# Chaining the transfer of E behind its batch's last tile transfer on the SyncE queue

## The chip, the cores and the metric

The kernel runs on one core of one Trainium2 chip, as one program in one launch. The metric is device time in microseconds (us): the median of several runs of one build. A profiled execution of the same program supplies the trace that is read below. Five engines work side by side: TensorE (PE; its weight loads are shown apart as PEld), VectorE (DVE), ScalarE (ACT), GpSimd (POOL) and SyncE (SP). In this kernel SP issues nearly all transfers, one after the other, in the order that the program was scheduled in; an issue whose semaphores are not yet there holds up every issue behind it.

## The reference

One layer of a hybrid decoder on 1056 tokens (1024 of a prompt, 32 of a sample group): a SwiGLU half, a mixing block (windowed attention beside a diagonal state-space model, the SSM), and a second SwiGLU half.

```python
x = x + 0.5 * swiglu(rms_norm(x, p['ffn1_norm']), p['ffn1_w1'], p['ffn1_w3'], p['ffn1_w2'])
h = rms_norm(x, p['mix_norm'])
...
y_ssm, new_re, new_im = s5_scan(u, s_re, s_im, p['ssm_a_re'], p['ssm_a_im'], p['ssm_log_dt'],
                                p['ssm_b_re'], p['ssm_b_im'], p['ssm_c_re'], p['ssm_c_im'], p['ssm_d'])
...
x = x + merged @ p['w_out']
x = x + 0.5 * swiglu(rms_norm(x, p['ffn2_norm']), p['ffn2_w1'], p['ffn2_w3'], p['ffn2_w2'])
```

The SSM has 32 groups of 64 complex states. Its discretised matrices depend on parameters alone, not on the tokens, so the kernel can work them out long before the scan needs them.

## The kernel before, in words

Each SwiGLU half is an up stage and a down stage. The up stage (`up`, lines 365 to 418) walks over 22 blocks of 128 hidden columns, f = 0 to 21 (the first two in another form, so the loop runs from f = 2). For each f, `wload` (282) asks SP for the weights `in_w3a` and `in_w1a` (line 286, two transfers each, into tiles `wr`), DVE forms sums of them (`ws`, `wr`), ACT casts the high parts (`wh`, line 301) and DVE the low parts (`wl`). PE then runs seven products for each of two column halves, 168 matmuls per f (line 232, into banks `P`), and DVE and ACT combine the results in tiles `e`; sums of them go to memory through `hs` (line 357). The down stage (`down`, 448) reads them back as `hl`.

The SSM's parameters are worked out inside the up stage of the first half, in NB = 8 batches, by the generator `params_b` (598 to 677). `hook` (681) drives it: at the end of f = 4, 6, ..., 18 it starts a batch, and its first part runs on POOL alone, behind a load of `tb` from `in_bc` (line 608). POOL forms B (in `ta`), C (in `tb`), and E, a table of powers that fills the right half of `ta` and is the last thing of the batch. Two f later, ahead of the last product of that f, the second part runs: PE transposes B (`ptr`, 638), ACT copies it to `mt` and SP stores that in `pa_d` (640); ACT copies C to `c` (647) and `cp` (652, stored by 653); PE multiplies (`pk`, 659); ACT copies to `kt` (662); eight small transfers spread `kt` into `tz` (672); ACT copies `tz` to `tp` (674), the batch's last tile; and two transfers store `tp` and E (`ta[:, 512:1024]`) in the left and right half of `pb_d` (675, 677). `pa_d` and `pb_d` are read by the scan, after the first half has ended.

What sets the order: each engine's instructions are put in order when the program is built, by a scheduler with its own timeline, which may place an instruction ahead of one that was written earlier. `tc.issue_after(ins)` adds an edge "behind ins in issue order" to the instructions of the block that run on the engine of `ins`, and to no others. Here `ins` is an ACT copy and the block holds only an SP transfer. `in_order(engine)` (142) chains the instructions of the block on the named engine one behind the other in issue order, without a wait for the end of any. It holds only instructions traced inside the block. The tiles `ta`, `tb`, `e`, `hl` and most others come from one pool of 34 buffers (NT); a new tile takes a buffer when its earlier reader or writer is through.

Of the kernel before, what the change touches and what calls it, by code (L numbers as in the profile page):

```python
# [46 lines left out]
def body(tc, I, O):  # L47
    nc = tc.nc
    V, S, Pl, PE = nc.vector, nc.scalar, nc.gpsimd, nc.tensor
    dma = nc.sync.dma_start  # L50
    mark = {}
    es = ExitStack()
    with es:
# [24 lines left out]
        def bank(pool_, name):  # L78
            p, n = psum[pool_]
            t = p.tile([128, n, 512] if n > 1 else [128, 512], F32, tag=pool_, name=name)  # L80
            return t
# [41 lines left out]
        def PP(shape, name, dt=F32):  # L123
            return pp_p.tile(shape, dt, tag="pp", name=name)
# [16 lines left out]
        @contextmanager  # L141
        def in_order(*engines, last=None):

            traced = nc.cur_bb.bb.instructions
            first = traced[-1]
            yield
            start = next(k for k in reversed(range(len(traced))) if traced[k] is first) + 1
            last = {} if last is None else last
            for i in traced[start:]:
                if i.engine in [e.engine for e in engines or (PE, V, S)]:  # L150
                    if i.engine in last:
                        tc.add_manual_dep(i, last[i.engine].name, mybir.DependencyInfo(
                            mybir.DependencyClass.NoSync, mybir.DependencyReason.DATA), reason="in_order")
                    last[i.engine] = i
# [345 lines left out]
        pb_d = dr.tile([NB, 128, 1024], F32, name="pb_d")  # L500
# [97 lines left out]
        def params_b(b):  # L598
# [69 lines left out]
            tz = PP([128, 4, 128], "tz")  # L668
# [2 lines left out]
            for j in range(8):  # L671
                dma(tv[:, j, :, j * 16:128], ktg[:, :, 0:(8 - j) * 16])
            tp = PP([128, 4, 16, 8], "tp")
            last = S.copy(tp, tz.rearrange("p g (j c) -> p g c j", j=8)).ins
            dma(pb_d[b, :, 0:512], tp.rearrange("p g c j -> p (g c j)"))
            with tc.issue_after(last):
                dma(pb_d[b, :, 512:1024], ta[:, 512:1024])

        todo, plast = [], {}
# [1 line left out]
        def hook(f, end):  # L681

            if not end:
                if f > 4 and f % 2 == 0:
                    with tc.issue_after(mark["pe"]):
                        next(todo.pop(), None)
                return
            if f == 2:
                with tc.issue_after(mark["hid"]):
                    load_consts()  # L690
                with tc.issue_after(mark["up"]):
                    params()
            elif f > 3 and f % 2 == 0 and f < 4 + 2 * NB:
                todo.append(params_b((f - 4) // 2))
                with in_order(Pl, last=plast):
                    next(todo[-1])
# [203 lines left out]
        for m0 in (0, 2):  # L900
# [5 lines left out]
            for c in range(NC):  # L906
                p = bank("pp", "pu")
# [706 lines left out]
```

## Time and profile before

| | us |
|---|---|
| median of 3 runs | 2124.15 |
| lowest, highest run | 2118.39, 2124.85 |
| the profiled execution, its own time | 2122.6 |
| its span, first to last instruction | 2120.8 |
| PE busy | 2041.1 (96%) |
| DVE busy | 1510.3 (71%) |
| ACT busy | 819.9 (39%) |
| POOL busy | 333.1 (16%) |

The 1.8 us between the profiled execution's time and its span lie outside the program's instructions. A busy PE is not a PE at its peak, since the duration of a matmul depends on the granted clock. "SPq" is SP's sequencer, that is, the queue of issues; the duration of an issue is not that of the transfer, and a DMA in the chain of waits is the transfer itself from issue to landing.

### The profile page before, as it was taken

The numbers are of one execution on the slowest core, as the hardware profiler recorded it, in microseconds if no ns is written. First come the engines' busy times: TensorE is split into PE (matmuls) and PEld (weight loads), VectorE is DVE, ScalarE is ACT, GpSimd is POOL, SyncE is SP. The second block draws the span as 40 slices with busy tenths as digits, with TensorE's granted clock in tenths as the row PEclk, the third lists the DMA queues.
The fourth block names the chain that finished last, engine by engine and source line by source line (L and its number), as shares of the span: only waits on it lengthen the run. The fifth ranks groups of instructions, "written<-read, shape, count | busy, mean of one in ns | idle before, by whom it ended". The sixth has DMA issues, their size and how long they took to land.

```text
span 2120.8 us, 39645 instructions
## 1 busy us (share of the span) xinstructions
PE 2041.1 (96%) x15588; PEld 2009.0 (95%) x15588; DVE 1510.3 (71%) x2566; ACT 819.9 (39%) x1569; POOL 333.1 (16%) x719
## 2 busy tenths in 40 slices
PE   8898989999999999999999899998999999999999
PEld 7898989998899999999999799988999999999999
DVE  5886766766477775767877856779777777756774
ACT  4432433333344452235555642344332232333342
POOL 0009777766000000320000200000000000000000
PEclk9899999999999999999999999999999999999999
DMA  4142333334777774652322274431432322377884
GB/s 164 36 150 99 117 100 100 100 115 143 269 260 258 266 270 142 204 167 64 91 77 97 80 264 141 136 104 40 152 106 77 122 91 92 103 263 245 301 281 159
DMA packets 155833, 320.64 MB, mean 151 GB/s; under 512 B 28592, under 2 KB 60144, under 8 KB 155632
## 3 DMA queue, kind: packets, MB, share of 16 engines
q1 hardware_dynamic: 155648, 318.12, 44.3%
q8 instruction: 122, 2.00, 0.4%
q14 instruction: 63, 0.52, 0.1%
HBM read 231.13 MB, written 84.07 MB: 149 GB/s over the span
## 4 chain that ended last, share of the span: by engine, by line
PE 75%; POOL 8%; DVE 7%; DMA 4%; issue 3%; ACT 2%; SPq 1%; DVEq 0%; ACTq 0%; POOLq 0%
PE P L232 27%; PE D L232 19%; PE pj L232 11%; POOL tb L84 6%; PE pm L232 4%; PE p L232 3%; PE pu L232 2%; PE Q L232 2%; POOL ta L84 2%; DMA hl<-hc 1%; DVE wl L84 1%; PE ss L735 1%; DVE B L96 1%; DMA tb<-in_bc 1%; DMA wr<-in_w1a 1%
## 5 line engine op out<-in xcount | busy, mean ns | idle before, releaser
L232 PE MATMUL P<-Xh,wh 128*128 128x264 f32 x2240 | 647.0, 289 | 38.0 <-DVE e L84 29.8
L232 PE MATMUL P<-Xl,wh 128*128 128x264 f32 x2240 | 644.6, 288 | 0.0
L232 PE MATMUL P<-Xh,wl 128*128 128x264 f32 x2240 | 641.9, 287 | 0.0
L232 PEld LDWEIGHTS P<-Xh,wh 128*128 128x128 f32 x2240 | 429.3, 192 | 44.1 <-DVE e L84 19.5
L232 PEld LDWEIGHTS P<-Xl,wh 128*128 128x128 f32 x2240 | 429.2, 192 | 1.7 <-issue 1.7
L232 PEld LDWEIGHTS P<-Xh,wl 128*128 128x128 f32 x2240 | 428.8, 191 | 0.2 <-issue 0.2
L232 PE MATMUL D<-hh,wh 128*128 128x264 f32 x1232 | 349.9, 284 | 1.9 <-DVE e L84 1.8
L232 PE MATMUL D<-hl,wh 128*128 128x264 f32 x1232 | 350.2, 284 | 0.7 <-DVE hl L84 0.7
L232 PE MATMUL D<-hh,wl 128*128 128x264 f32 x1232 | 349.1, 283 | 0.7 <-DVE wl L84 0.7
L84 DVE TENSOR_TENSOR wl<-wr,wh 128x512 fp32r<-128x512 f32 (+1 forms) x426 | 289.0, 694 | 60.9 <-ACT wh L301 41.8
L211 ACT CAST wh<-wr 128x512 fp32r<-128x512 f32 (+1 forms) x266 | 154.1, 606 | 317.2 <-DVE wr L84 158.4
L84 DVE TENSOR_TENSOR e<-e,P 128x528 f32<-128x528 f32 (+1 forms) x250 | 169.7, 680 | 116.2 <-PE P L232 85.6
L232 PEld LDWEIGHTS D<-hh,wh 128*128 128x128 f32 x1232 | 231.9, 188 | 2.5 <-ACT wh L211 1.4
L232 PEld LDWEIGHTS D<-hh,wl 128*128 128x128 f32 x1232 | 231.5, 188 | 1.3 <-DVE wl L84 1.3
L232 PEld LDWEIGHTS D<-hl,wh 128*128 128x128 f32 x1232 | 231.6, 188 | 1.1 <-DVE hl L84 1.1
L301 ACT CAST wh<-wr 128x512 fp32r<-128x512 f32 x160 | 98.9, 620 | 275.5 <-PE P L232 264.7
L232 PE MATMUL pj<-xh,wh 128*128 128x352 f32 x528 | 172.1, 326 | 3.0 <-DVE gt L84 3.0
L232 PE MATMUL pj<-xl,wh 128*128 128x352 f32 x528 | 171.4, 325 | 0.0
L232 PE MATMUL pj<-xh,wl 128*128 128x352 f32 x528 | 171.1, 324 | 0.0
L301 ACT CAST wh<-ws 128x512 fp32r<-128x512 f32 x120 | 74.4, 621 | 222.3 <-PE P L232 214.5
L84 DVE TENSOR_TENSOR wr<-wr 128x512 f32<-128x512 f32 (+1 forms) x140 | 123.8, 885 | 31.2 <-DMA wr<-in_w2b 15.6
L84 DVE TENSOR_TENSOR hl<-hl,hh 128x1056 fp32r<-128x1056 f32 x84 | 97.6, 1162 | 33.8 <-ACT hh L427 33.7
(608 smaller groups left out, 3698.8 us busy)
## 6 DMA issues: line engine op xcount, KB each, us to landing
hl<-hc SPq DMA_DIRECT2D x70, 528.0 KB, 5.6
wr<-in_w2a SPq DMA_DIRECT2D x60, 512.0 KB, 5.2
wr<-in_w2b SPq DMA_DIRECT2D x60, 512.0 KB, 4.7
hc<-hs SPq DMA_DIRECT2D x110, 264.0 KB, 3.1
wr<-in_w_in SPq DMA_DIRECT2D x26, 512.0 KB, 3.5
hc<-e SPq DMA_DIRECT2D x42, 264.0 KB, 3.5
wr<-in_w3a SPq DMA_DIRECT2D x40, 256.0 KB, 3.0
wr<-in_w1a SPq DMA_DIRECT2D x40, 256.0 KB, 4.7
```

What stands on the lines that cost most here:

```text
L84: e.tensor_tensor(out=o, in0=a, in1=b, op=op)
L96: V.scalar_tensor_tensor(out=o, in0=a, scalar=s, in1=b, op0=op0, op1=op1)
L211: S.copy(h[:, 0:m, :], r[:, i:i + m, :])
L232: mark["pe"] = PE.matmul(ps, a, b, start=first and i == 0, stop=last and i == 2, **kw).ins
L301: S.copy(h, s)
L735: PE.matmul(ps, f32(ones), s[:, kk, :], start=a + i + kk == 0, stop=a == 1 and i + kk == 2)
```

## The change

The two stores of a batch are put into a block that chains SP's instructions: first the store of `tp`, then that of E. The hold on ACT's copy, which named no SP instruction, is gone.

```diff
             tp = PP([128, 4, 16, 8], "tp")
-            last = S.copy(tp, tz.rearrange("p g (j c) -> p g c j", j=8)).ins
-            dma(pb_d[b, :, 0:512], tp.rearrange("p g c j -> p (g c j)"))
-            with tc.issue_after(last):
+            S.copy(tp, tz.rearrange("p g (j c) -> p g c j", j=8))
+            with in_order(nc.sync):
+                dma(pb_d[b, :, 0:512], tp.rearrange("p g c j -> p (g c j)"))
                 dma(pb_d[b, :, 512:1024], ta[:, 512:1024])
```

Two places of SP's queue show what moves. The first is ahead of the weights of f = 7, where batch 0 is at work; the semaphores that an issue waits for stand in brackets, among them one DMAHW, that of the transfer eight places earlier. Before (`ta_1733` is batch 0's E, `mt` its first stored tiles):

```order
L357 DMA hc1_136<-hs_2047 128x528 [waits DMAHW5_49,DVE_49]
L677 DMA pb_d_124<-ta_1733 128x512 [waits DMAHW6_49,Pool_49]
L286 DMA wr_3017<-in_w3a 128x512 [waits DMAHW7_49,DVE_49]
L286 DMA wr_3017<-in_w3a 128x512 [waits DMAHW0_49]
L640 DMA pa_d_123<-mt_2252 128x256 [waits DMAHW1_49,Activation_49]
L640 DMA pa_d_123<-mt_2258 128x256 [waits DMAHW2_49,Activation_49]
L286 DMA wr_3016<-in_w1a 128x512 [waits DMAHW3_49,DVE_49]
```

With the change:

```order
L357 DMA hc1_136<-hs_2047 128x528 [waits DMAHW5_49,DVE_49]
L286 DMA wr_3017<-in_w3a 128x512 [waits DMAHW6_49,DVE_49]
L286 DMA wr_3017<-in_w3a 128x512 [waits DMAHW7_49]
L640 DMA pa_d_123<-mt_2252 128x256 [waits DMAHW0_49,Activation_49]
L640 DMA pa_d_123<-mt_2258 128x256 [waits DMAHW1_49,Activation_49]
L286 DMA wr_3016<-in_w1a 128x512 [waits DMAHW2_49,DVE_49]
```

Batch 0's E, with its wait for POOL, has left the place ahead of the weights of f = 7 and of batch 0's own `pa_d` stores.

The second place is the end of batch 0, ahead of the weights of f = 8 (`ta_2336` is batch 1's E, `tb_2940` the load that opens batch 2). Before:

```order
L675 DMA pb_d_124<-tp_2302 128x512 [waits DMAHW0_49,Activation_49]
L286 DMA wr_3257<-in_w3a 128x512 [waits DMAHW1_49,DVE_49]
L286 DMA wr_3257<-in_w3a 128x512 [waits DMAHW2_49]
L677 DMA pb_d_124<-ta_2336 128x512 [waits DMAHW3_49,Pool_49]
L286 DMA wr_3256<-in_w1a 128x512 [waits DMAHW4_49,DVE_49]
L286 DMA wr_3256<-in_w1a 128x512 [waits DMAHW5_49]
L357 DMA hc4_134<-hs_2613 128x528 [waits DMAHW6_49,DVE_49]
L405 DMA hc5_138<-e_2455 128x528 [waits DMAHW7_49,DVE_49]
L608 DMA tb_2940<-in_bc 128x128 [waits DMAHW0_49]
```

With the change:

```order
L676 DMA pb_d_124<-tp_2302 128x512 [waits DMAHW7_49,Activation_49]
L677 DMA pb_d_124<-ta_1733 128x512 [waits DMAHW0_49,Pool_49]
L286 DMA wr_3257<-in_w3a 128x512 [waits DMAHW1_49,DVE_49]
L286 DMA wr_3257<-in_w3a 128x512 [waits DMAHW2_49]
L286 DMA wr_3256<-in_w1a 128x512 [waits DMAHW3_49,DVE_49]
L286 DMA wr_3256<-in_w1a 128x512 [waits DMAHW4_49]
L357 DMA hc4_134<-hs_2613 128x528 [waits DMAHW5_49,DVE_49]
L405 DMA hc5_138<-e_2455 128x528 [waits DMAHW6_49,DVE_49]
L608 DMA tb_2940<-in_bc 128x128 [waits DMAHW7_49,DMAHW0_49]
```

Batch 1's E no longer stands ahead of batch 2's load; batch 0's does, behind `tp` of batch 0. That load also waits for DMAHW0 now, E's own landing, since its tile takes over the buffer that E was read from. So it goes on to the last batch: before, the E that is issued near `tp` of a batch is that of the next batch, which POOL is still working on; with the change it is that batch's own. POOL's order is the same in both; PE, DVE and ACT change by a few neighbouring places near f = 21 and in the attention.

## Rows read from the trace of the kernel before

**Rows 1.** The page's chain that ended last: share of the span by engine.

```profile
PE 75%; POOL 8%; DVE 7%; DMA 4%; issue 3%; ACT 2%; SPq 1%; DVEq 0%; ACTq 0%; POOLq 0%
```

**Rows 2.** Windows: length, busy us (count) of PE PEld DVE ACT POOL, PEclk, DMA, GB/s.

```profile
239.77:284.81 45.04, 45.04 (x369) 44.24 (x368) 32.51 (x49) 18.38 (x38) 33.74 (x74) 1.00 0.31 101
...
205.84:555.71 349.87, 322.92 (x2532) 315.09 (x2532) 231.77 (x343) 131.62 (x273) 233.10 (x519) 0.97 0.37 120
98.97:555.71 456.74, 427.35 (x3361) 418.13 (x3362) 319.93 (x541) 165.11 (x337) 275.61 (x617) 0.97 0.37 119
...
1484.15:1892.68 408.53, 406.37 (x3324) 405.80 (x3325) 294.53 (x450) 121.99 (x204) 0.00 (x0) 0.99 0.35 120
```

**Rows 3.** Waits of PE from 205 to 556: us in total, times, longest.

```profile
PE P L232 <- DVE e L84: 21.4, 9, 3.5
PE pk L659 <- ACT c L647: 5.5, 1, 5.5
```

**Rows 4.** Chain of waits in time, 235 to 300: start us, us, what.

```profile
242.07 5.18 DMA tb<-in_bc
...
247.39 1.19 POOL tb L84 x2
...
266.55 0.04 POOL ta L627
...
284.81 0.33 SPq L677
...
287.09 4.60 DMA wr<-in_w1a
...
...
293.12 3.06 PE P L232 x23
```

**Rows 5.** Waits of SP's queue from 186 to 556.

```profile
SPq L677 <- POOL ta L84: 137.8, 8, 20.7
SPq L286 <- DVE wl L84: 43.9, 12, 7.1
```

**Rows 6.** Waits of POOL from 205 to 556.

```profile
POOL tb L84 <- DMA tb<-in_bc: 56.1, 6, 10.8
```

**Rows 7.** Timeline of SP, 204 to 245: start us, us, queue, line, operation, out<-in.

```profile
205.84 0.32 SPq L677 DMA_DIRECT2D pb_d<-ta  x1
...
215.32 5.12 SPq L672 DMA_DIRECT2D tz<-kt  x8
222.83 0.33 SPq L675 DMA_DIRECT2D pb_d<-tp  x1
...
239.77 0.33 SPq L677 DMA_DIRECT2D pb_d<-ta  x1
```

**Rows 8.** Timeline of ACT, 180 to 350; in brackets the idle time before.

```profile
210.53 0.87 ACT L647 COPY c<-tb 64x288 f32<-64x288 f32 x2 [7.67 <-DMA pa_d<-mt]
...
250.79 0.64 ACT L639 COPY mt<-ptr 128x256 f32<-128x256 f32 x2
...
265.56 1.11 ACT L674 COPY tp<-tz 128x512 f32<-128x512 f32 x1 [1.02 <-DVE wl L84]
```

**Rows 9.** Chain of waits in time, 500 to 600.

```profile
523.20 6.87 DMA hl<-hc
...
533.18 4.70 PE P L232 x24
537.88 0.44 PE ptr L638 x4
...
542.45 0.54 PE pk L659 x4
```

**Rows 10.** DVE by line and shape, 205 to 520 (POOL at work): count, busy us, mean ns.

```profile
L84 DVE TENSOR_TENSOR e<-e,P 128x528 f32<-128x528 f32 x78 | 54.6, 701 | 32.8 <-PE P L232 21.1 <-issue 6.0 <-ACT e L105 1.9
L84 DVE TENSOR_TENSOR wl<-wr,wh 128x512 fp32r<-128x512 f32 x54 | 41.7, 772 | 16.7 <-ACT wh L301 16.7
```

**Rows 11.** The same view, 1500 to 1890 (POOL idle).

```profile
L84 DVE TENSOR_TENSOR wl<-wr,wh 128x512 fp32r<-128x512 f32 x77 | 52.9, 687 | 21.7 <-ACT wh L301 20.9 <-ACT wh L211 0.8
```

## The prediction

> **What bounds the kernel now.** I read the page's chain first: TensorE carries 75% of what ended last and POOL 8% [rows 1]. POOL is no arithmetic engine of the large products, so 8% of the chain on it is the thing to find. Windows show where. The up stage of the first half takes 456.74 us from a place early in f = 2 to its last product, that of the second half, between the same two places and with no SSM work, 408.53 us [rows 2]. The SSM's own PE work explains little: four transposes in 0.44 us and twice four `pk` in 0.54 us [rows 9], 1.52 us a batch, 12.2 us in eight. The rest, 48.2 - 12.2 = **36.0 us**, is loss. From 205.84 us on PE is idle for 349.87 - 322.92 = 26.95 us [rows 2], and ten waits, 21.4 + 5.5 us, are all of it [rows 3]. The other 9 us are slower matmuls: the granted clock averages 0.97 of 2.4 GHz there, falling after such waits, and is 1.00 in the one stretch without any [rows 2].
>
> The chain in time tells what stands behind the waits. Batch 2's load is issued at 242.07; POOL starts 5.2 us later and works to the end of E; at that moment, 284.81, SP's issue of E is released; the weights `in_w1a` leave at 287.09 and take 4.60 us; DVE makes `e` from what follows, and PE starts again at 293.12 after an idle stretch [rows 4]. So SP stands still in front of E, eight times, for 137.8 us in all, at most 20.7 us, and everything behind it is late: weights, stores and also the load for the next batch. While they are issued and land, POOL has nothing to do: 56.1 us in six waits [rows 6]. It is a ring: POOL's batch, then E, then the next load, then POOL. A turn, from E at 239.77 [rows 7] to E at 284.81, takes 45.0 us, while PE needs 408.53 / 10 + 1.5 = 42.4 us for the two f of a turn (20 f in the stretch). POOL sets the pace of PE, through the queue.
>
> **The change, part by part.**
>
> *The wait in front of E.* E of batch b moves behind `tp` of batch b, hence about one turn later. POOL is through with batch 0 at 205.84 and `tp` of batch 0 goes at 222.83 [rows 7], so this E waits for nothing even there, and in later turns it has a turn's length to spare. The 137.8 us of SP's waiting go. They are no gain by themselves: SP would have waited part of that for free `wr` buffers (43.9 us of such waits are there already [rows 5]). The gain is in what PE waits for.
>
> *First batch.* The weights of f = 7 and the `pa_d` stores stand behind E no longer. ACT waited 7.67 us for those stores [rows 8], and PE for ACT 5.5 us [rows 3]. Taken whole: **5.5 us**.
>
> *Later batches.* Nine waits of PE for `e`, 21.4 us [rows 3]. One of them, that ended at 533.18, follows a load of `hl` that itself takes 6.87 us [rows 9] and belongs to the step into the down stage; I leave its 3.5 us. The others follow late weights, as the one at 293.12 does. Taken: **17.9 us**.
>
> *Clock.* With 23.4 of 26.95 us of idling gone, the slow stretches behind them go as well: of 9 us, part of which lies ahead of 205, I take **6 us**.
>
> *What is added.* SP's wait for `tp` was hidden behind E and is now met first. ACT's `tz` to `tp` copy starts 14.8 us after that batch's `mt` copy [rows 8], and in batch 0 SP stood from the last small transfer, 215.32 + 5.12, to 222.83 before `tp`, 2.4 us [rows 7]. Waits before E of 137.8 / 8 = 17 us [rows 5] cost PE about 21.4 / 8 = 2.7 us each [rows 3], so a wait of 2.4 us should stay hidden by weights that were asked for earlier. Bounds: 0, or 2.4 us in each of eight turns, 19; I take 0.4 each, near the first, **3 us**. Below nothing it cannot go, as it is a wait added. The `in_bc` load now waits for E's landing too; the two stand six other issues apart, and a load of that kind lands within 5.2 us [rows 4], so at most some 3 us of SP's time, which I count in the same 3. The number of issues is the same.
>
> *POOL later?* Batch b + 2's load now follows E of batch b, so POOL could be late for PE's transposes, which stand in PE's order. By the rows: `tp` comes 16 us after `mt` of the same batch [rows 8], the next load followed it by 19.2 us even with E's wait between (242.07 [rows 4] - 222.83 [rows 7]), it lands in 5.2 us, and B and C are done 19.2 us after POOL's start (266.55 - 247.39 [rows 4]): 60 us after `mt` of batch b at most. The second part of b + 2 comes two turns after that `mt`, 84.8 us. Some 25 us are left over. E is done 37.4 us after POOL's start (284.81 - 247.39), long before its new issue. Nothing.
>
> **Sum:** 5.5 + 17.9 + 6 - 3 = 26.4 us, say 26. Against the profiled execution, 2122.6 - 26 = 2096.6; that execution stands 1.55 us under the median of the runs, so on the median's scale 2124.15 - 26 = **2098 us**. Less than 0.3%, 6.4 us, either way is about what a measurement of this kernel can tell from no change. The bounds of the sum are a gain of 36.0 us (all of the loss: 2088) and one of 5.5 + 17.9 - 19 = 4.4 us (nothing from the clock, every `tp` wait in full: 2120).
>
> **The rivals.**
>
> *A. VectorE and POOL get in each other's way.* If PE no longer idles, DVE's work is packed closer while POOL runs, and DVE's `e` stays late. For it: the same `wl` takes 772 ns while POOL works [rows 10] and 687 ns while it does not [rows 11], 12% more, and it is DVE that PE waits for. Against: in 239.77:284.81, with POOL busy for 33.74 and DVE for 32.51 of 45.04 us, PE had no idle time and the clock was 1.00 [rows 2]; at a turn of 42.4 us DVE would be at 77%. If half of idle and clock stays, the gain is 12 us: 2112. Taken to the end, the two would take strict turns: 33.7 us of POOL and, without the DVE work that reads PSUM (`e<-e,P`, 54.6 of 315 us [rows 10], here 7.8 us), 24.7 us of DVE make 58 us a turn; PE would then be paced by that sum in both kernels, and the time would be 2124 again. The trace has that work in a turn of 45 us, so it speaks against it: 0.03 for the strict form, 0.2 for A. The Trainium skill ("SBUF — State Buffer", section "SBUF: two separate sides") states the strict form, an exclusive lock on a port pair that VectorE and GpSimd share, held for a whole instruction. By that rule the change would win nothing; by these rows the busy spans overlap, and 12% on some instructions is what is left of it.
>
> *B. The change does not do what it says.* SP's wait only takes another name: without E it stands as long before `wr` buffers that DVE frees, and weights arrive as before. For it: such waits are there, 12 of them, up to 7.1 us [rows 5]. Against: the ring shows POOL's end, not a buffer, ahead of the weights [rows 4]. Gain within 0.3%: 2123. Chance 0.03.
>
> *C. Slower: POOL starts too late.* The load of batch b + 2 sits behind `tp` and E of batch b, and if `tp` were late by a whole f (21 us) and the issues after it by 14 more, B and C would not be ready when PE reaches its transposes; PE would then wait in every turn from batch 2 on. It decides from about 25 us of delay, the margin above. At 10 us beyond it, six waits of 10 us less the 26 us won make 34 us more: 2158. Nothing in the rows delays `tp` by that much. Chance 0.04.
>
> **How the numbers follow.** The forecast, a gain of 17 to 36 us, has 0.7; A 0.2; strict turns and B 0.06 together; C 0.04. The forecast's own range is 2088 to 2107; A and the lower bound of the sum reach up to 2120, but thinly over 2114. With 2 us below for the spread between runs, the range is 2086 to 2114, which leaves out strict turns, B, C and the edge of A. Faster by over 0.3%: forecast and A, 0.9. Within: 0.06. Slower: 0.04.
>
> **What the profile of the changed kernel would show.** Right: SP's wait for POOL in front of E near zero instead of 137.8 us; PE's wait of 5.5 us for `c` gone and at most two or three waits for `e` left in the up stage; that stage 425 to 440 us long instead of 456.74; POOL's share of the chain down from 8% to almost none; POOL waiting for `in_bc` still, since PE now sets its pace. Wrong: waits of SP for `wr` buffers grown by over 100 us with PE's waits unchanged (B); PE's waits for `e` at 10 us or more with DVE busy throughout (A); PE waiting at `ptr` or `pk` for POOL in every batch (C).

## The result and the profile after

The changed kernel takes **2085.51 us** (median of 4 runs, 2084.0 to 2086.6) against 2124.03 us of the kernel before in the same series: ratio 0.983, 95% interval 0.9817 to 0.9844. The forecast was 2098 us with a range of 2086 to 2114: faster, as forecast, by 38.5 us instead of 26, and half a microsecond under the range's lower end. The profiled execution takes 2086.6 us with a span of 2084.8; its span is 36.0 us shorter than that of before.

The page's chain of the changed kernel, by engine, to be set against [rows 1]:

```profile
PE 89%; DVE 6%; ACT 2%; issue 2%; DMA 1%; SPq 0%; ACTq 0%; DVEq 0%
```

POOL has left the chain, PE went from 75% to 89%, and transfers from 4% to 1%. What PE waited for from 200 to 540 us, where [rows 3] had 26.9 us in ten waits:

```profile
PE D L232 <- ACT wh L211: 1.3, 1, 1.3
PE D L232 <- DVE e L84: 0.9, 1, 0.9
PE D L232 <- DVE hl L84: 0.4, 1, 0.4
PE D L232 <- DVE wl L84: 0.2, 1, 0.2
```

All four belong to `D`, the down stage. In the up stage no wait is left, not for `c`, not for `e`, and not the one at 533 us that the prediction left standing. SP's queue from 180 to 540 us, against [rows 5]:

```profile
SPq L286 <- DVE wl L84: 114.4, 20, 11.6
SPq L676 <- ACT tp L674: 21.0, 8, 3.5
...
SPq L677 <- POOL tb L84: 1.9, 4, 0.8
```

The wait in front of E fell from 137.8 to 1.9 us. SP still stands still for much of that time: some 70 us more for `wr` buffers that DVE frees, and 21.0 us for `tp`. These waits cost PE nothing, since they are those of a queue that is ahead of the work: a buffer comes free because its weights are used up, and the next ones still arrive in time. The chain of waits in time shows PE's turn:

```profile
243.34 4.15 PE P L232 x34
249.75 35.88 PE P L232 x294
286.06 4.15 PE P L232 x34
```

A turn is 286.06 - 243.34 = 42.72 us (worked out beforehand: 42.4), where POOL's ring took 45.0 in the turn that the prediction read and 46.8 on average, (520.4 - 239.77) / 6 from the issues of E; and it repeats to within 0.02 us from 207 to 506 us. POOL on its timeline, in which a bracket is the idle time before:

```profile
189.29 0.10 POOL L627 MEMSET ta<- 128x2 f32 x1
...
336.35 0.10 POOL L627 MEMSET ta<- 128x2 f32 x1
...
358.71 0.44 POOL L84 TENSOR_TENSOR tb<-tb,par 128x32 f32<-128x32 f32 x2 [5.41 <-issue]
...
400.83 0.44 POOL L84 TENSOR_TENSOR tb<-tb,par 128x32 f32<-128x32 f32 x2 [6.56 <-issue]
...
444.20 0.44 POOL L84 TENSOR_TENSOR tb<-tb,par 128x32 f32<-128x32 f32 x2 [7.38 <-issue]
```

The MEMSET of line 627 opens E, once a batch. Over the first four turns POOL runs at its own pace, (336.35 - 189.29) / 4 = 36.8 us a batch, and gets ahead of PE; from then on it waits 5 to 7 us at the head of a batch. The profile names no releaser there; the load was issued 2.1 to 2.8 us before, at 356.1, 398.7 and 441.4, so it is most likely still the load that POOL waits for, now because PE's turn had not come to it. Before, it waited there because its own E held that load up [rows 6].

**Where the time came from.** Three windows of the kernel before: the whole up stage, from the place in f = 2 to the first product of the down stage; a piece of its end; and a stretch with POOL at work throughout (columns as in [rows 2]):

```profile
98.97:563.99 465.02, 434.74 (x3420) 425.34 (x3421) 323.57 (x547) 167.36 (x340) 276.03 (x619) 0.97 0.38 123
...
555.71:563.99 8.28, 7.39 (x61) 7.21 (x61) 3.64 (x6) 2.25 (x3) 0.42 (x2) 1.00 0.93 306
...
205.84:520.00 314.16, 290.69 (x2285) 283.82 (x2285) 215.42 (x318) 118.99 (x244) 232.54 (x518) 0.97 0.34 110
```

The same stage, and the same stretch of time, of the changed kernel:

```profile
99.33:525.33 426.00, 422.68 (x3420) 415.63 (x3421) 321.94 (x547) 167.97 (x340) 271.74 (x620) 0.99 0.40 134
...
205.84:520.00 314.16, 314.16 (x2561) 308.56 (x2560) 230.02 (x344) 131.49 (x270) 229.52 (x522) 1.00 0.39 131
```

With the same 3420 matmuls the stage is 39.0 us shorter. PE's idle time went from 465.02 - 434.74 = 30.3 us to 3.3: 27.0 us. Its busy time fell by 12.1 us, because a matmul takes less at the granted clock of 1.00: in the common stretch 314.16 / 2561 = 122.7 ns against 290.69 / 2285 = 127.2 ns. In these two profiled executions the rest of the program is 3.0 us longer, hence 36.0 us of span; where was not looked for.

The granted clock says why the matmuls were slower. In the changed kernel it is 1.00 from 205.84 to 520 us. In the kernel before, six stretches between 205 and 556 us stand at its lower level, 0.50 or 1.2 GHz. Each begins within a wait of PE or right behind one, though not every wait has one. The one behind the wait of 2.77 us that ended at 346.36:

```profile
346.70:349.90 3.20, 3.20 (x17) 3.20 (x16) 2.00 (x3) 0.65 (x1) 2.90 (x6) 0.50 0.93 283
```

Together they make 23.9 us, and half of that, 12 us, is what PE lost in them.

### The profile page after: what moved, and what is told of

The parts are those of the page before. It is cut to its first block, busy times and chain, and to the rows that moved or that the text cites. A ratio compares the mean times of both kernels' runs of the same rounds, so it can differ in the third digit from the quotient of the medians.

```text
span 2084.8 us, 39651 instructions
## 1 busy us (share of the span) xinstructions
PE 2030.5 (97%) x15588; PEld 2001.1 (96%) x15588; DVE 1507.8 (72%) x2566; ACT 820.7 (39%) x1569; POOL 327.8 (16%) x719
## 4 chain that ended last, share of the span: by engine, by line
PE 89%; DVE 6%; ACT 2%; issue 2%; DMA 1%; SPq 0%; ACTq 0%; DVEq 0%
PE P L232 39%; PE D L232 20%; PE pj L232 11%; PE pm L232 4%; PE p L232 4%; PE pu L232 2%; PE Q L232 2%; PE pg L232 1%; PE ss L735 1%; DVE wl L84 1%; DMA hl<-hc 1%; DVE B L96 1%; DVE Xl L84 1%; PE po L1206 1%; PE sc L1167 1%
## 5 line engine op out<-in xcount | busy, mean ns | idle before, releaser
L232 PEld LDWEIGHTS P<-Xh,wh 128*128 128x128 f32 x2240 | 424.4, 189 | 20.8 <-ACT e L380 9.4
L232 PEld LDWEIGHTS P<-Xl,wh 128*128 128x128 f32 x2240 | 424.0, 189 | 1.7 <-issue 1.7
L232 PEld LDWEIGHTS P<-Xh,wl 128*128 128x128 f32 x2240 | 424.1, 189 | 0.0
```

The costliest lines, as they stand in the source:

```text
L232: mark["pe"] = PE.matmul(ps, a, b, start=first and i == 0, stop=last and i == 2, **kw).ins
```

## The experiments

The theory under test: the cost of the kernel before is a ring, E's wait for POOL holds up the load that POOL needs next and the weights that PE needs next. The rivals: the cost is E's transfer itself or its place beside other transfers; only some of the eight waits matter; POOL is off the path whatever it does. A run's time is compared with runs of the kernel before on the same chip.

**1. Only batch 0's E chained.** `in_order(Pl)` names an engine that issues nothing in the block, so the other batches are not held and their E goes early, as before.

```diff
-            with in_order(nc.sync):
+            with in_order(*((nc.sync,) if b == 0 else (Pl,))):
```

> Only batch 0's E is chained behind its tp; the other seven stay early. Ring theory (POOL's batch, E, the next in_bc load, POOL again set the pace of every turn): POOL's batches 1 to 7 start where they did, so PE's 5.5 us wait goes at first and comes back as longer waits for weights later; the gain is 0 to 3 us, 2121 to 2124 us, and the last E is issued at about 520 us as before. Rival, each wait of PE costs its own length: 5.5 us and about 1.7 us of slow clock are won for good, 2117 us, with the other nine waits at 21.4 us in all unchanged.

Measured: 2121.12 us against 2119.6, ratio 1.0003 (0.9993 to 1.0013), no gain. The waits of PE in the up stage:

```profile
PE P L232 <- DVE e L84: 26.6, 11, 5.5
```

The waits of SP in front of E, now seven:

```profile
SPq L677 <- POOL ta L84: 127.4, 7, 19.1
```

The longest wait of PE on its timeline:

```profile
245.20 0.59 PE L232 MATMUL P<-Xh,wh 128*128 128x264 f32 x1 [5.50 <-DVE e L84]
```

PE's 5.5 us wait for `c` is gone, as the prediction's first term says, and a wait of 5.50 us for `e` stands at 245 instead. The sum of PE's waits is 26.6 us, where it was 26.9. A stall taken out ahead of a ring that runs slower than PE is no gain: PE meets the ring sooner and waits there.

**2. Only the last batch's E chained** (`b == NB - 1` in the same line).

> Only batch 7's E is chained. The up stage keeps its ring until the last batch. If the late start of the down stage's first loads behind batch 7's E was the cause of the last wait of 3.5 us and of the 5.0 us that the step into the down stage lost: both go, 8 to 9 us in all, 2115 us, with the earlier waits unchanged. Rival, those 5.0 us came from the changed pace of the whole stage: 0 to 4 us, 2120 to 2124 us.

Measured: 2118.67 us, ratio 0.9988 (0.9976 to 1.0000), between the two expectations and hardly to be told from no change. Waits of PE:

```profile
PE P L232 <- DVE e L84: 20.0, 9, 2.9
PE pk L659 <- ACT c L647: 6.0, 1, 6.0
```

The wait at 533 us is gone, and the up stage is 4.6 us shorter (460.4 against 465.0), not more. That wait was the last E's doing, not that of the step into the down stage. Neither end of the ring is worth much alone; the gain comes when the ring is broken in every turn.

**3. The wait kept, the transfer gone late.** The changed kernel, with a last column of E sent to a scratch tensor as soon as E is made (an early transfer that waits for POOL, as E's did).

```diff
+            dma(ew_d[b], ta[:, 1023:1024])
```

> E is chained as in the change, and one column of E (128 x 1, 512 bytes instead of 256 KB) is sent besides at the place where E stood before. If the wait for POOL in the queue is the whole cost, SP waits some 130 us in front of the small transfer and the time is that of the kernel before, 2120 to 2128 us. Rival, E's transfer itself (its bytes or its buffer) was what hindered: the time of the changed kernel, 2083 to 2090 us.

Measured: 2172.09 us, ratio 1.024 (1.0222 to 1.0258), 52 us longer than the kernel before and beyond either expectation. The wait came back, but so did something else. The chain in time, 225 to 350:

```profile
288.23 10.84 DMA pb_d<-ta
...
342.34 11.63 DMA pb_d<-ta
```

E's own transfer, 2.7 us in the changed kernel, takes 11 us behind a transfer of 128 rows of 4 bytes, and the `in_bc` load waits for its landing. So this run tells nothing of the wait alone; the next one does.

**4. The same with a block of 128 columns.** The edit is that of 3 with `ta[:, 896:1024]`, rows of 512 bytes.

> As the run with one column, but the early transfer is a block of 128 columns (64 KB in rows of 512 bytes), so that its landing takes a usual time. E itself stays chained as in the change. If the wait for POOL in the queue is the whole cost: SP waits 120 to 140 us in front of the block, E lands within 4 us, a turn of the up stage is 45 to 48 us and the time 2118 to 2140 us. Rival, E's own transfer at the early place was the hindrance: 2083 to 2095 us.

Measured: 2126.16 us against 2121.52, ratio 1.0024 (1.0012 to 1.0037), though E itself goes late. The waits of SP in front of the block:

```profile
SPq L634 <- POOL ta L84: 135.2, 8, 19.1
```

The waits of PE:

```profile
PE P L232 <- DVE e L84: 25.1, 11, 6.1
PE pk L661 <- ACT c L649: 5.9, 2, 5.6
```

All kinds of waits of before are back with a quarter of E's bytes in the early place, and the whole gain is lost. The wait is the cost, not E's transfer.

**5. E early, but POOL's loads four batches ahead.** The kernel before in the order of its transfers, but `in_bc` has a buffer of its own for four batches, so POOL's next load does not stand behind E. Two lines of the edit; the rest makes room, by putting three constants into the same buffer later on.

```diff
+            for b_ in range(0 if not b else b + 3, min(b + 4, NB)):
+                dma(bcs[b_ % 4], I["bc"][b_])
```

> E stays early as in the kernel before, but in_bc is loaded up to four batches ahead into a buffer of its own, so that POOL's next batch does not wait for a load that stands behind E. Ring theory: POOL runs its batches with no wait for in_bc (56 us before), gets ahead by about 5 us a turn, SP's wait in front of E falls from 137.8 us to 40 to 70 us, most waits of PE after batch 2 go: 2090 to 2102 us, with the 5.5 us wait of batch 0 still there. Rival, a wait of SP ahead of weights is enough by itself and the load's place does not matter: PE's waits stay near 27 us, 2115 to 2126 us.

Measured: 2099.35 us, ratio 0.990 (0.988 to 0.992). The waits of SP:

```profile
SPq L284 <- DVE wl L84: 88.9, 17, 11.7
SPq L677 <- POOL ta L84: 42.6, 8, 12.6
```

The waits of PE in the up stage:

```profile
PE pk L659 <- ACT c L647: 5.7, 1, 5.7
PE P L230 <- DVE e L84: 4.8, 1, 4.8
```

This cuts the ring at its other place. POOL no longer waits for a load, so it is done sooner and SP waits 42.6 us for it instead of 137.8; PE's nine waits shrink to one of 4.8 us. That alone gives about 21 us of the gain, so more than half of the loss came through POOL's load. The other 14 us stand with E in its early place; that they go through the weights behind it is what the two waits left suggest, and was not tried apart.

**6 and 7. One more POOL step a batch, in both kernels.** The last doubling of E's powers is done twice, with the same result.

```diff
-            for m in range(7):
+            for m in (0, 1, 2, 3, 4, 5, 6, 6):
```

In the kernel before:

> The kernel before, with the last doubling step of E worked out twice on POOL, six more instructions of 0.4 to 0.9 us in each batch, some 3.2 us. Ring theory: each of seven turns and the first wait get that much longer, 22 to 26 us in all: 2138 to 2150 us. Rival, POOL does not set the pace and the queue only happens to be late: 2117 to 2127 us.

In the changed kernel:

> The changed kernel with the same doubled step. If POOL has left the path, as E is now issued a turn after it is done: no change, 2083 to 2089 us, and POOL's batch of about 41 us still fits in a turn of 42.7 us. Rival, POOL is now just as close to the pace and shares VectorE's port: 2095 to 2112 us.

Measured: before with the step 2139.43 us, ratio 1.0085 (1.0063 to 1.0108), 18 us more; the changed kernel with it 2085.11 us, ratio 0.9827 (0.9802 to 0.9851), nothing. Waits of PE in the first:

```profile
PE P L232 <- DVE e L84: 35.4, 11, 7.4
PE pk L659 <- ACT c L647: 8.4, 1, 8.4
```

A window of the second:

```profile
205.84:520.00 314.16, 314.16 (x2561) 308.69 (x2561) 233.25 (x343) 130.74 (x268) 262.05 (x570) 1.00 0.39 131
```

Before, most of each batch's extra step reaches the end of the program, 18 / 8 = 2.3 us a turn: POOL is on the path. After, POOL is busy for 262.05 us instead of 229.52 in the stretch, and PE has no idle time at all.

**8. E issued by ACT.** The hold of before, on ACT's copy, with the transfer on ACT's own queue, where it holds.

```diff
             with tc.issue_after(last):
-                dma(pb_d[b, :, 512:1024], ta[:, 512:1024])
+                S.dma_start(pb_d[b, :, 512:1024], ta[:, 512:1024])
```

> E is issued from ACT's queue behind ACT's copy of tp, where the hold on that copy does act, and no longer from SP at all. If the early place in SP's queue was the whole cost, it does not matter where the late issue stands: 2083 to 2090 us, with eight more issues of about 0.4 us on ACT hidden by its idle time, and SP's wait for tp alone left. Rival, ACT's casts are delayed enough to hold PE: 2090 to 2100 us.

Measured: 2083.46 us, ratio 0.9827 (0.9804 to 0.9849), as the changed kernel. On ACT's timeline E follows its copy at once:

```profile
213.34 1.12 ACT L674 COPY tp<-tz 128x512 f32<-128x512 f32 x1 [0.16 <-ACT wh L301]
213.36 0.35 ACTq L677 DMA_DIRECT2D pb_d<-ta  x1
```

Either queue will do; the late place is what counts. It agrees with the reading that the hold of before held nothing because it named an engine that issues no part of its block.

**9 and 10. Four and ten more POOL steps in the changed kernel.** The edit of 6 with the last step done five and eleven times. How slow may POOL become?

> The kernel with the change, with the last doubling step of E done five times instead of once, so that POOL does four more steps a batch. In the profile of the changed kernel POOL starts the two small MEMSETs of E, which follow B and C, at 189.3 us in batch 0 and at 462.1 us in batch 7: 39.0 us a batch at its own pace, against a turn of 42.7 us of PE. With one more step the same two stood at 188.7 and 472.9, 40.6 us a batch; with one more step in the kernel before the time rose by 18 us in eight turns, 2.25 us a turn. Four more steps make 45 to 48 us a batch, 3 to 5 us more than a turn. Theory (PE sets the pace only as long as POOL's batch is shorter than a turn, and POOL's lead at batch 0, about 10 us from those MEMSETs to PE's transposes at 200, is used up first): over seven turns POOL falls behind by 18 to 38 us, less about 10 us of lead and some 8 us for B, which is done that much ahead of the MEMSETs: 0 to 20 us, so 2085 to 2106, with PE waits at the transposes or at `pk` in the last batches alone. Rival (POOL is off the path, whatever it does): 2083 to 2088 and no such wait. Second rival (the wait of SP in front of E comes back as soon as POOL is late, and costs as before): SP waits for POOL at the store of E by over 60 us, and PE waits for `e` in many turns, 2110 to 2125.

> As the run before, with ten more steps a batch instead of four: POOL's batch is 39.0 us plus ten times 1.6 to 2.25 us, 55 to 61.5 us, 12 to 19 us more than PE's turn of 42.7 us. Theory (POOL sets the pace again, now without the queue between): it falls behind by 86 to 132 us in seven turns, less some 18 us of lead: 68 to 114 us more, 2154 to 2200; PE waits in nearly every batch from the third on, at the transposes (for B) or at `pk` (for C), or for `e` behind SP's wait for POOL in front of E. Rival (POOL is off the path): 2083 to 2090.

Measured: 2138.97 us (ratio 1.008, 1.0063 to 1.0097) with four, 2258.96 us (1.0644, 1.0629 to 1.066) with ten. With four, the MEMSETs of line 627 (count, ns, first and last start):

```profile
L627 POOL MEMSET ta<- x8: 98/102/104, 187.9 to 537.2; 128x2 f32 x8
```

The waits of PE from 200 to 780:

```profile
PE P L232 <- DVE e L84: 23.2, 9, 4.2
PE P L232 <- ACT e L380: 14.2, 3, 13.2
```

The waits of SP in front of E:

```profile
SPq L677 <- POOL ta L84: 103.2, 7, 17.3
```

The chain by line from 430 to 545:

```profile
by line: POOL tb L84 65.9%; POOL ta L84 24.5%; issue 9.5%; POOL ta L628 0.1%; POOL ta L627 0.1%; POOLq L84 0.1%
```

With ten steps, the MEMSETs:

```profile
L627 POOL MEMSET ta<- x8: 98/101/102, 188.5 to 652.1; 128x2 f32 x8
```

And the waits of SP in front of E:

```profile
SPq L677 <- POOL ta L84: 219.5, 7, 34.2
```

Rival "off the path" falls: from 430 to 545 us the chain is POOL and the gaps between its instructions, nothing else. My size for four steps (2085 to 2106) was wrong, that for ten fell 59 us short at its upper end. POOL's batch is (537.2 - 187.9) / 7 = 49.9 us with four steps and 66.2 with ten, against 36.8 without: 2.9 to 3.3 us a step, not 1.6 to 2.25. I had divided by the mean spacing of the MEMSETs, 39.0 us, in which POOL's waiting in the last turns is counted. With four steps PE's turns, from the first to the last transposes (198.6 to 537.9), take 48.5 us instead of 42.8, seven times 5.7 = 40 us. PE has no wait at the transposes or at `pk`; it waits for `e`, with SP standing in front of E. That is the mechanism of the second rival, the wait in front of E come back, with a larger price. The other 13 us are one wait of PE, 13.2 us, that ends at 564.52, ahead of the last E (573.0). The chain leads from POOL's last instruction through ACT to it, and ACT stood before the cast of the down stage's first operand:

```profile
562.05 0.63 ACT L427 CAST hh<-hl 128x528 fp32r<-128x528 f32 x1 [17.95 <-POOL ta L84]
```

Nothing that this cast reads comes from POOL; that its new tile takes over a buffer of the last batch, from the pool of 34, is the likely reason and was not tested. No rival had named it. The two runs lie 53.5 and 173.5 us above the changed kernel, 20.0 us for each step between four and ten; the line meets the changed kernel's time at 4 - 53.5 / 20.0 = 1.3 steps. By this estimate POOL may grow by about one step a batch before it costs anything, and experiment 7 had that one.

## Why the prediction was right, and where its sizes were off

**The mechanism was right.** The ring of POOL, E and load set PE's pace; experiment 4 puts the wait back with a quarter of the bytes and gets the loss back, 5 cuts the ring at the load and wins half of it, and 6 and 7 show POOL on the path before and off it after. The share of POOL in the chain, the 137.8 us in front of E, the wait for `c` and those for `e` went as the last part of the prediction said. POOL still waits for `in_bc`, as it said too, but for 19.4 us in three waits instead of 56.1 in six.

**The step that failed is the first number of the loss, 36.0 us.** It was taken from a window that ended at 555.71, "to its last product". There the chain leaves PE for a transfer, but PE's last product of the stage ends with the first of the down stage at 563.99: the window behind 555.71 has 61 matmuls, and PE busy for 7.39 of 8.28 us. The counts of [rows 2] would have shown it: 3324 matmuls in the second half and 12 of the SSM in each of eight batches make 3420, not 3361, so the two windows were not the same stretch of work. The stage is 465.0 us long, and the loss was 465.0 - 408.5 - 12.2 = 44.3 us. What had been called the bound of the gain, 36 us, was below what came.

**Term by term,** against the 39.0 us of the stage:
- *First batch and later waits, 5.5 + 17.9 = 23.4.* All went. The split is not one of independent terms: experiment 1 takes the first 5.5 us out and they come back at the next turn. The 3.5 us at 533 us that were left as the load of `hl`'s doing went too (experiment 2), so 27.0 us of idling.
- *Clock, 6.* It was 12.1 us. Of the loss, 36.0 - 26.95 = 9 us had been put to slow matmuls with a part ahead of 205; with the right end of the stage more falls to them, and the rows ahead of 205 changed little. The whole lies where PE no longer idles: half of the 23.9 us at 0.50.
- *`tp`, -3.* It cost nothing: 21.0 us of waiting in eight, at most 3.5, all hidden by weights that had been asked for earlier, as the near end of its bounds had it. SP's timeline shows the order that was forecast, E right behind `tp` and the load some 11.7 us behind E:

```profile
215.71 0.32 SPq L676 DMA_DIRECT2D pb_d<-tp  x1
216.13 0.38 SPq L677 DMA_DIRECT2D pb_d<-ta  x1
...
227.84 0.38 SPq L608 DMA_DIRECT2D tb<-in_bc  x1
```

So 26.4 + 3.5 + 6.1 + 3 = 39.0 us.

**POOL later: nothing,** was right, with a margin of another kind than the 25 us given. A single delay may be that long; in a steady run what counts is the pace, and there POOL's 36.8 us stand against PE's 42.7. Experiments 9 and 10 go beyond it, and the kernel is slower than before at four steps.

**Rival A** (DVE and POOL in each other's way) falls as a forecast of the time: from 205.84 to 520 us of the changed kernel DVE is busy for 230.02 us and POOL for 229.52, with no idle time of PE. The argument that the prediction set against its strict form does not hold, though, and that its 0.03 came out well was luck. The prediction added up busy times, and a busy span of POOL can hold waiting. POOL and DVE in the changed kernel, the same POOL instruction twice:

```profile
235.62 0.69 DVE L84 TENSOR_TENSOR ws<-wr 128x512 f32<-128x512 f32 x1
...
235.76 0.66 POOL L84 TENSOR_TENSOR ta<-tb 128x32 f32<-128x32 f32 x1
...
237.12 0.70 DVE L84 TENSOR_TENSOR e<-e,P 128x528 f32<-128x528 f32 x1
237.41 0.25 POOL L84 TENSOR_TENSOR ta<-tb 128x32 f32<-128x32 f32 x1
```

Beside a DVE instruction that reads PSUM (`e<-e,P`) it takes 0.25 us; beside one that reads SBUF alone (`ws<-wr`) it takes 0.66 and ends 0.1 us behind it. DVE pays as well: the `wl` that took 772 ns in [rows 10] takes 734 here, and 687 with POOL idle [rows 11].

```profile
L84 DVE TENSOR_TENSOR wl<-wr,wh 128x512 fp32r<-128x512 f32 x59 | 43.3, 734 | 10.5 <-ACT wh L301 9.3 <-ACT wh L211 0.4
```

The exclusive lock of the Trainium skill ("SBUF — State Buffer", section "SBUF: two separate sides") would let the two take turns, and on single instructions the trace looks like that. It does not settle the strict form. At the lengths that the same instructions have undisturbed (an estimate, from their medians over five of the traces) the turn from 239.77 to 284.81 holds some 23 us of POOL and 22 of the DVE work that does not read PSUM, not 33.7 and 24.7: 45 in 45.0 us, which turns would allow. The 299 us from 207.03 to 506.05 of the changed kernel hold 163 and 150, together 14 us more than there is time, so there the two overlap by a little.

**Rival B** had its sign, `wr` waits up by some 70 us, without its consequence: PE's waits did not stay. **Rival C** did not happen, and experiments 9 and 10 come nearest to it, though PE waits there for `e` and not at `ptr` or `pk`: the point from which it decides is POOL's pace, not a delay of the load.

## What to carry to other kernels

In a queue that issues in order, a store that waits for a slow producer also holds up the loads of that producer and of everyone else; if the producer's next load stands behind it, the queue and the producer make a ring whose turn is their sum. Put such a store where its data is surely there already, behind something that comes a turn later, and look at whether a hold names the engine that issues the transfer. Read the pace that each engine could keep by itself from turns in which it does not wait, and the end of a stage from the engine's own instructions, not from where the chain happens to leave it. Before adding up the busy times of two engines, look at what the same instruction takes undisturbed: a busy span can hold waiting.

## What the runs showed of the hardware that was not expected

A transfer of 128 rows of 4 bytes, half a kilobyte in all, is not small in its effect: with it the E transfer of 256 KB two issues behind took 10.8 and 11.6 us in the chain instead of 2.7 us, and the time was 46 us longer than with a block of 64 KB in rows of 512 bytes in its place (2172.09 against 2126.16 us). What of it is the transfer and what the longer turn that follows was not taken apart.

The same POOL step had no one price: (472.9 - 188.7) / 7 - 36.8 = 3.8 us in the changed kernel with one more, 3.3 with four, 2.9 with ten. Over the turns of these runs DVE was busy for 74, 69 and 51% of the time, and in the one stretch of the run with four in which DVE stood idle (544.84 to 562.71 us) a step took 2.7 us, from 555.27 to 558.00. So the price falls with DVE's work beside it, as the two lengths of one POOL instruction under rival A suggest; no run changed DVE's work alone.
